# Twelve output-projection steps by block sums in place of ten, and a step's three weight sums in two vector operations

## The chip, the cores and the metric

The kernel runs on one NeuronCore of a Trainium2 chip. Its engines work side by side, each through its own queue in order: TensorE (PE: products; PEld in the profile is its loading of the stationary operand), VectorE (DVE), ScalarE (ACT), GpSimd (POOL) and SyncE (SP), which here only issues transfers. The metric is the device time of one execution in microseconds; runs of one kernel are given with their median.

## The reference

One layer over 256 tokens of width 2048: a normed gated linear attention with its output projection, then a squared-ReLU MLP with 8192 hidden units, then a final norm. Cut to what matters:

```python
h = h + gla(rmsnorm(h)) @ w_out                 # w_out: 2048 x 2048
a = relu(rmsnorm(h) @ w_up)                      # w_up: 2048 x 8192
h = h + (a * a) @ w_down                         # w_down: 8192 x 2048
return rmsnorm(h)
```

All is float32. The kernel splits each weight and each activation into a high part and a low part and forms high x high, low x high and high x low, so that one product of the reference is three products on TensorE.

## The kernel before, in words

The input projections come first (some 288 us), then the output projection (288 to 376 us), then the MLP (376 us to the end).

**The output projection.** `out_group(g, ...)` computes 512 of the 2048 output columns; there are four groups. A group walks over the 2048 input rows in eight steps of 256 rows, in the order `ORDER = (3, 0, 2, 1, 4, 7, 5, 6)`; I call a step by its number kp. A step's weights are a tile `raw` of 128 x 1024: four blocks of 256 columns (row half 0: blocks 0 and 1; row half 1: blocks 2 and 3). A step is done in one of two ways.

- A plain step: one load of 512 KB, one cast to the high part (`copy_hi`, ACT, line 118), one low part (DVE, line 131), then 24 products of 128 x 256 (8 pairs of a stationary and a moving block, three products each).
- A step by sums, a seven-product scheme for a 2 x 2 block product (Strassen's, in the form with few additions): two loads of 256 KB, and an accumulating transfer from POOL's queue that adds block 1 onto block 0 in the tile; a cast and a low part of blocks 1 to 3 (768 columns) and 9 products from them; then three additions on DVE in the same tile (lines 743 to 745), a second cast in two pieces, a second low part (line 761), and 12 products of the sums. That is 7 pairs, 21 products. The second half is held back in `pending` and runs after the next step's products.

The activations need sums too: `turn_pair` makes eight blocks (four sums, four originals; `form_sums`) for the row pairs in `FORMED = (0, 1, 7)`. `summed(g)` says which steps of a group go by sums: 0 and 1 in the first and the last group, 0, 1 and 7 in the two between, ten in all. At the last such step the banks of the sums are copied to `comb` (ACT, lines 767 and 768), combined by four DVE additions (769 to 772), and after the last step two DVE additions (775) write `h`.

**Set in the order of the work.** Each group also turns the last group's `h` by PE transposes at its step 1, copies `h` into the banks of the next group at step 3 (`begin_out`), and squares the last group's `h` at step 4 (`ssq_h`). The high and low parts live in five slots each, taken in turn, so a cast waits until PE has done with the high part five before; `raw` has six buffers. PE's order is fixed by `then_mm`; the order in which ACT and DVE take their work in the output projection is chosen by the compiler's scheduler under a few ordering rules, and each engine then keeps to it. In the MLP `copy_hi` orders ACT's casts too.

**The MLP.** `up` and `down` are generators that alternate: an up step (24 products; low part on DVE at line 165) and a down step, of which 112 of 120 in the interleaved part go by sums in the same way (additions at lines 1088 to 1090, second low part at 1129). The first up steps run alone, right after the output projection. Beside them the last group's `h` is squared (ACT 780), reduced (DVE 803, 804), its root is taken on POOL (356), and DVE writes two diagonals of it, one for each half of the tokens (810, `scale2_diagonals`). PE then makes a row of them (`last_turn`, line 818) and turns the last quarter of `h`. `last_turn` is the ninth entry of `side`, and an up step takes two entries, so PE meets it in the middle of the high products of up step 4.

Of the kernel before, what the change touches and what calls it, by code (L numbers as in the profile page):

```python
# [32 lines left out]
P = 128  # L33
T = 256
# [34 lines left out]
def tile_gla_mlp(ctx, tc, x, xt, cols, w_vg, w_in, w_gate, w_out, w_up, w_down, final_norm, out):  # L69
# [516 lines left out]
                nc.scalar.activation(s, acc[t][c], AF.Silu, scale=r1[:, t : t + 1])  # L586
                nc.vector.tensor_tensor(on[:, t, lo : lo + 512], on[:, t, lo : lo + 512], s, op=ALU.mult)

    S3, S1, S2, S4, A12, A11, A22, A21 = range(8)

    def form_sums(f, sub):
        sub(f[:, S3 : S1 + 1], f[:, A21:].to_broadcast([P, 2, P]), f[:, A11 : A22 + 1])
        sub(f[:, S2], f[:, A11], f[:, S1])
        sub(f[:, S4], f[:, A12], f[:, S2])

    FORMED = (0, 1, 7)
    in_forms = lambda a: a.rearrange("p (f s) -> p f s", f=8)
# [2 lines left out]
    def turn_pair(kp, bank, gain, to):  # L600

        raw_form = raw_forms[kp == 1]
        for i in range(2):
            s = bank[:, i * T : (i + 1) * T].rearrange("p (t s) -> p t s", t=NT)
            nc.scalar.activation(raw_form[:, A12 + 1 - i :: 2], s, AF.Copy, scale=gain(2 * kp + i))
        form_sums(raw_form, lambda o, x, y: nc.vector.tensor_tensor(o, x, y, op=ALU.subtract))
        nc.scalar.copy(to[0], raw_form)
        nc.vector.tensor_tensor(to[1], raw_form, to[0].bitcast(F32), op=ALU.subtract)

# [89 lines left out]
    def out_group(g, order, summed, between):  # L699

        tt = nc.vector.tensor_tensor
        banks = [out_banks[g, t] for t in range(NT)]
        sums_banks = []
        begun = set()
        pending = None
        block = lambda i, n=1: slice(i * T, (i + n) * T)

        def product(bank, o, a, w, n, last=False):
            for x in a[: 2 - n]:
                for d in range(0, w.shape[-1], T):  # L710
                    newest[0] = nc.tensor.matmul(
                        bank[:, o + d : o + d + T], x, w[:, d : d + T],
                        start=bank in sums_banks and bank.name not in begun, stop=last, skip_group_check=True,
                    ).ins
                    begun.add(bank.name)

        def products(these, w, last=False):
            with then_mm():
                for n in range(2):
                    for bank, o, a, c in these:  # L720
                        product(bank, o, a, w[n][:, c], n, last and n == 1)

        for step, kp in enumerate(order):
            by = kp in summed
            raw = raw_tile()[:, : 2 * GT]
            src = w_out[2 * kp * P : 2 * (kp + 1) * P, g * GT : (g + 1) * GT].rearrange("(i p) c -> p i c", p=P)
            if by:
                for i in range(2):
                    last_load[0] = nc.sync.dma_start(out=raw[:, i * GT : (i + 1) * GT], in_=src[:, i])
                nc.gpsimd.dma_start(out=raw[:, :T], in_=src[:, 0, T:], accum_op=ALU.add)  # L730
            else:
                last_load[0] = nc.sync.dma_start(out=raw.rearrange("p (i c) -> p i c", i=2), in_=src)
            w = parts(raw, 2 * GT, slots(), [(T * by, 2 * GT)])
            if by:
                if not sums_banks:
                    sums_banks.extend(psum_bank(i) for i in out_ids[4:])
                f = forms_o(kp)
                at = lambda k, f=f: [a[:, k] for a in f]
                p16, p57 = sums_banks
                products([(p16, 0, at(A11), block(1)), (banks[0], T, at(A12), block(3)), (banks[0], 0, at(S4), block(2))], w)  # L740
                u = raw.rearrange("p (f s) -> p f s", f=4)
                with tc.issue_after(last_lo[0].ins):
                    tt(u[:, 2], u[:, 0], u[:, 2], op=ALU.add)
                    tt(u[:, 1], u[:, 2], u[:, 1], op=ALU.subtract)
                    last = tt(u[:, 3], u[:, 2], u[:, 3], op=ALU.add)
            else:
                for t, i in ((0, 0), (0, 1), (1, 0), (1, 1)):
                    products([(banks[t], 0, row_o(2 * kp + i, t), block(2 * i, 2))], w, step == len(order) - 1 and i == 1)
            if pending:
                pending()  # L750
                pending = None
            if step in between:
                with tc.issue_after(last_hi[0].ins), tc.issue_after(last_lo[0].ins), then_mm():
                    between[step]()
            if by:
                def pending(u=raw, at=at, final=kp == [k for k in order if k in summed][-1]):
                    to = slots()
                    for c in (0, GT):
                        copy_hi(to[0][:, c : c + GT], u[:, c : c + GT])
                    with tc.issue_after(last_lo[0].ins):  # L760
                        last_lo[0] = tt(to[1][:, :G], u, to[0][:, :G].bitcast(F32), op=ALU.subtract)
                    products([
                        (p57, 0, at(S1), block(0)), (p57, T, at(S3), block(1)),
                        (p16, T, at(S2), block(2)), (banks[1], T, at(A22), block(3)),
                    ], to, final)
                    if final:
                        nc.scalar.copy(comb[:, 1:3], two(p16))
                        nc.scalar.copy(comb[:, 0:4:3], two(p57))
                        tt(comb[:, 2], comb[:, 1], comb[:, 2], op=ALU.subtract)
                        tt(comb[:, 0], comb[:, 0], comb[:, 2], op=ALU.subtract)  # L770
                        tt(comb[:, 4], comb[:, 0], comb[:, 3], op=ALU.add)
                        tt(comb[:, 5], comb[:, 2], comb[:, 3], op=ALU.subtract)
        for t in range(NT):
            o = h[:, t, g * GT : (g + 1) * GT].rearrange("p (f s) -> p f s", f=2)
            tt(o, two(banks[t]), comb[:, 4 * t : 4 * t + 2], op=ALU.add)

    def ssq_h(g):
# [3 lines left out]

    ORDER = (3, 0, 2, 1, 4, 7, 5, 6)
    newest[0] = None
    summed = lambda g: FORMED if 0 < g < GROUPS - 1 else FORMED[:2]
    out_group(0, ORDER, summed(0), {
        1: lambda: (turn(on, turned_o, gain_o, 2), turn(on, turned_o, gain_o, 3, forms_o, spare_out(0))),
        3: lambda: begin_out(1),
    })
    hth, htl = (big.tile([P, KT, T], F32R, tag="A" + i, name="h" + i, bufs=1) for i in "hl")
    turned_h = lambda kt: [a[:, kt, :].rearrange("p (t s) -> p t s", t=NT) for a in (hth, htl)]  # L790
    for g in range(1, GROUPS):
        out_group(g, ORDER, summed(g), {
            1: lambda: turn(h, turned_h, g2, g - 1), 4: lambda: ssq_h(g - 1),
            **({3: lambda: begin_out(g + 1)} if g + 1 < GROUPS else {}),
        })
# [126 lines left out]
    def on_vector(i):  # L922
        newest_form[1] = i.ins
# [30 lines left out]
    def forms(m, kp, s):  # L954
        f = form
        on_act(nc.scalar.activation(
            f[:, A12:].rearrange("p (t i) s -> p i t s", t=2), s.rearrange("p i (t s) -> p i t s", t=2), AF.Square
        ))
        if True in ways_of(m, kp):
            form_sums(f, lambda o, x, y: on_vector(nc.vector.tensor_tensor(o, x, y, op=ALU.subtract)))  # L960

    def form_parts(m, kp, act):
        ways = ways_of(m, kp)
# [55 lines left out]
    def down(passes):  # L1019
# [7 lines left out]
        for n, (m, g) in enumerate(passes):  # L1027
# [12 lines left out]
            for kp in range(KP):  # L1040
# [40 lines left out]
                if by_parts:  # L1081
                    these = (P16, 0, at(A11), block(1)), (B32, T, at(A12), block(3)), (B32, 0, at(S4), block(2))
                    u = raw.rearrange("p (f s) -> p f s", f=4)
                    tt = nc.vector.tensor_tensor


                    with tc.issue_after(last_lo[0].ins):
                        tt(u[:, 2], u[:, 0], u[:, 2], op=ALU.add)  # L1088
                        tt(u[:, 1], u[:, 2], u[:, 1], op=ALU.subtract)  # L1089
                        last_sum[0] = tt(u[:, 3], u[:, 2], u[:, 3], op=ALU.add).ins  # L1090
                else:
                    these = [
                        (k, 0, at(f[i]), block(2 * i, 2))
# [15 lines left out]
                def of_sums(u=raw, products=products, at=at, kp=kp, banks=banks, quick=fresh and quick, g=g, then=ahead_of):  # L1109
# [8 lines left out]
                            banks[P57] = begin(P57, g)  # L1118
                    if then and by_sums(*then, 0):
                        ahead = {k: begin(k, then[1]) for k in (B32, P16)}  # L1120
                    for c in (0, GT):
                        copy_hi(to[0][:, c : c + GT], u[:, c : c + GT])
                    if quick and kp == 0:
                        settle(P57)
                        banks[BX4] = begin(BX4, g)
# [1 line left out]
                        settle(BX4)  # L1127
                    with tc.issue_after(last_lo[0].ins):
                        last_lo[0] = nc.vector.tensor_tensor(to[1][:, :G], u, to[0][:, :G].bitcast(F32), op=ALU.subtract)  # L1129
                    early = (P57, 0, at(S1), block(0)), (P57, T, at(S3), block(1))  # L1130
                    late = (P16, T, at(S2), block(2)), (BX4, T, at(A22), block(3))
                    products(0, early, to)
                    yield
                    products(0, late, to)
# [32 lines left out]
    def combine(g):  # L1167
# [4 lines left out]
        def put(t):  # L1172
            hv = h[:, t, g * GT : (g + 1) * GT].rearrange("p (i s) -> p i s", i=2)
            nc.vector.tensor_tensor(hv, hv, e[:, :2], op=ALU.add)  # L1174

        return [
            tt(2, 1, 2, ALU.subtract), tt(0, 0, 2, ALU.subtract), lambda: put(0),
            tt(1, 2, 3, ALU.subtract), tt(0, 0, 3, ALU.add), lambda: put(1),
        ]

    passes = [(m, g) for m in range(ROUNDS) for g in order_of(m) if m < ROUNDS - 1 or g < 2]
# [130 lines left out]
```

## Time and profile before

| | |
|---|---|
| runs | 1044.98 us median of 3 (1044.53 to 1045.18) |
| the profiled execution | 1045.44 us, of which the span from the first to the last instruction is 1043.7 us |
| mean granted TensorE clock | 0.998 |
| busy: PE, DVE, ACT, POOL | 1035.2, 871.1, 721.7, 117.8 us |
| output projection by sums | 10 steps of 32; accumulating transfers 10 |

A busy time is a share of the span only on average: the stages differ. In a row of the timeline stand the start, the time, the engine, the line, the operation, the tiles (out, then in) and how many instructions are merged; in square brackets the time the engine stood idle before, and what released it. PE and DVE overlap one instruction's end with the next one's start, so distances between starts are shorter than durations.

### The profile page before, as it was taken

What the parts mean: (1) busy time and instruction counts of PE and PEld (TensorE: products, weight loads), DVE (VectorE), ACT (ScalarE), POOL (GpSimd) and SP (SyncE); (2) the same over time, 40 slices, a digit from 0 to 9 for tenths busy, and PEclk for the clock granted to TensorE, in tenths of its full rate; (3) what the DMA queues carried; (4) which work ended last, traced back from release to release, by engine and by line L of the source; (5) the groups of instructions that cost most, each with busy time, mean ns of one, the idle gap of its engine ahead of it and who ended that gap; (6) DMA issues with size and microseconds to landing.
All of it is one profiled execution on the core that took longest, in us unless ns stands there. A gap on an engine that the chain in (4) does not pass through costs nothing. (4 is left out here: it accounts for less than half of the span.)

```text
span 1043.7 us, 23272 instructions
## 1 busy us (share of the span) xinstructions
PE 1035.2 (99%) x9064; PEld 1034.3 (99%) x9064; DVE 871.1 (83%) x1287; ACT 721.7 (69%) x1084; POOL 117.8 (11%) x161
## 2 busy tenths in 40 slices
PE   9999999999999999999999999999999999999997
PEld 9999999999999999999999999999999999999997
DVE  5768644656498866889999999999999999999887
ACT  6785544546477755678678688778778777777785
POOL 0000000010011001111111111111111111111100
PEclk9999999999999999999999999999999999999999
DMA  9957665556666686678887887887888888887782
GB/s 333 334 174 208 197 195 170 152 152 182 175 204 189 209 256 190 179 210 226 228 247 230 236 235 217 239 236 223 246 232 222 249 230 228 231 227 225 233 244 89
DMA packets 118414, 226.53 MB, mean 217 GB/s; under 512 B 10608, under 2 KB 26864, under 8 KB 118176
## 3 DMA queue, kind: packets, MB, share of 16 engines
q1 hardware_dynamic: 100064, 207.39, 63.5%
q0 software_dynamic: 17568, 16.00, 10.3%
q8 instruction: 71, 1.16, 0.4%
q10 hardware_dynamic: 672, 1.66, 0.4%
q14 instruction: 39, 0.32, 0.1%
HBM read 222.91 MB, written 2.10 MB: 216 GB/s over the span
## 5 line engine op out<-in xcount | busy, mean ns | idle before, releaser
L118 ACT CAST hi<-raw 128x512 fp32r<-128x512 f32 (+4 forms) x630 | 499.5, 835 | 263.0 <-DVE raw L1089 73.0
L131 DVE TENSOR_TENSOR lo<-raw,hi 128x768 fp32r<-128x768 f32 (+3 forms) x226 | 238.7, 1061 | 90.9 <-ACT hi L118 88.4
L855 PE MATMUL acc<-hi,act 128*128 128x256 f32 x1696 | 247.9, 276 | 0.0
L855 PE MATMUL up<-hh,hi 128*128 128x256 f32 x1024 | 238.8, 277 | 0.0
L855 PE MATMUL up<-hl,hi 128*128 128x256 f32 x1024 | 238.7, 276 | 0.0
L165 DVE TENSOR_TENSOR lo<-raw,hi 128x1024 fp32r<-128x1024 f32 x160 | 195.0, 1221 | 29.9 <-ACT hi L118 29.5
L855 PEld LDWEIGHTS acc<-hi,act 128*128 128x128 f32 x1696 | 217.7, 188 | 0.0
L855 PEld LDWEIGHTS up<-hl,hi 128*128 128x128 f32 x1024 | 192.3, 188 | 0.0
L855 PEld LDWEIGHTS up<-hh,hi 128*128 128x128 f32 x1024 | 192.3, 188 | 0.0
L1065 POOL DMA_DIRECT2D raw<-in_w_down x112 | 97.1, 867 | 518.6 <-DMA raw<-in_w_down 229.8
L1129 DVE TENSOR_TENSOR lo<-raw,hi 128x1024 fp32r<-128x1024 f32 x112 | 136.7, 1220 | 1.3 <-ACT hi L118 1.0
L855 PE MATMUL up<-hh,lo 128*128 128x256 f32 x1024 | 137.0, 276 | 0.0
L855 PE MATMUL acc<-lo,act 128*128 128x256 f32 x848 | 134.1, 276 | 0.0
L855 PEld LDWEIGHTS up<-hh,lo 128*128 128x128 f32 x1024 | 125.7, 188 | 0.0
L855 PEld LDWEIGHTS acc<-lo,act 128*128 128x128 f32 x848 | 113.5, 188 | 0.0
L176 PE MATMUL acc<-hi,xA 128*128 128x256 f32 (+1 forms) x728 | 105.5, 279 | 0.2
L176 PEld LDWEIGHTS acc<-hi,xA 128*128 128x128 f32 x728 | 93.8, 188 | 0.7 <-ACT hi L118 0.6
L176 PE MATMUL acc<-lo,xA 128*128 128x256 f32 (+1 forms) x364 | 60.9, 278 | 0.1
L176 PEld LDWEIGHTS acc<-lo,xA 128*128 128x128 f32 x364 | 50.3, 188 | 0.3 <-DVE lo L131 0.3
L1088 DVE TENSOR_TENSOR raw<-raw 128x256 f32<-128x256 f32 x112 | 47.5, 424 | 2.9
L1089 DVE TENSOR_TENSOR raw<-raw 128x256 f32<-128x256 f32 x112 | 47.5, 424 | 2.8
L219 PE MATMUL acc<-xA,hi 128*128 128x256 f32 x288 | 49.2, 276 | 0.0
(185 smaller groups left out, 1281.9 us busy)
## 6 DMA issues: line engine op xcount, KB each, us to landing
raw<-in_w_up SPq DMA_DIRECT2D x128, 512.0 KB, 4.6
raw<-in_w_down SPq DMA_DIRECT2D x224, 256.0 KB, 4.4
raw<-in_w_in SPq DMA_DIRECT2D x80, 512.0 KB, 3.7
raw<-in_w_down POOLq DMA_DIRECT2D x112, 128.0 KB, 5.1
raw<-in_w_out SPq DMA_DIRECT2D x22, 512.0 KB, 4.7
raw<-in_w_down SPq DMA_DIRECT2D x16, 512.0 KB, 4.8
raw<-in_w_vg SPq DMA_DIRECT2D x14, 520.0 KB, 8.4
raw<-in_w_out SPq DMA_DIRECT2D x20, 256.0 KB, 3.4
```

What stands on the lines that cost most here:

```text
L118: last_hi[0] = nc.scalar.copy(to, raw)
L131: last_lo[0] = nc.vector.tensor_tensor(lo[:, s], raw[:, s], hi[:, s].bitcast(F32), op=ALU.subtract)
L165: last_lo[0] = nc.vector.tensor_tensor(to[1], dst, to[0].bitcast(F32), op=ALU.subtract)
L176: nc.tensor.matmul(o[:, m], x, w[:, m], start=first and c == 0, stop=last, skip_group_check=True)
L219: nc.tensor.matmul(o, u[:, i, s], m, start=kt == 0 and n == 0 and j % 2 == 0, stop=kt == KT - 1 and n == 2, skip_group_check=True,)
L855: newest[0] = nc.tensor.matmul(o, x, w, start=first, stop=last, skip_group_check=True).ins
L1065: nc.gpsimd.dma_start(out=raw[:, :T], in_=src[:, 0, T:], accum_op=ALU.add)
L1088: tt(u[:, 2], u[:, 0], u[:, 2], op=ALU.add)
L1089: tt(u[:, 1], u[:, 2], u[:, 1], op=ALU.subtract)
L1129: last_lo[0] = nc.vector.tensor_tensor(to[1][:, :G], u, to[0][:, :G].bitcast(F32), op=ALU.subtract)
```

## The change

Three things are changed together.

- `summed` is gone: all four groups take steps 0, 1 and 7 by sums, twelve in place of ten. The activation sums of pair 7 were made before too.
- The scheme is written with other signs. `weight_sums` forms block 2 as block 0 minus block 2 in one DVE operation, and blocks 1 and 3, each minus the new block 2, in one operation over two blocks of 256 with the subtrahend repeated. The activation sums (`form_sums`) and the combinations change signs and places, with as many operations as before.
- The second cast takes blocks 0 and 2 first, then 1 and 3 (before: 0 and 1, then 2 and 3), and the products of blocks 0 and 2 come first. The same stands in the MLP's down steps.

```diff
-    S3, S1, S2, S4, A12, A11, A22, A21 = range(8)
-    def form_sums(f, sub):
-        sub(f[:, S3 : S1 + 1], f[:, A21:].to_broadcast([P, 2, P]), f[:, A11 : A22 + 1])
-        sub(f[:, S2], f[:, A11], f[:, S1])
-        sub(f[:, S4], f[:, A12], f[:, S2])
+    S3, S2, S1, S4, A12, A11, A22, A21 = range(8)
+    def form_sums(f, tt):
+        tt(f[:, S3], f[:, A21], f[:, A11], ALU.subtract)
+        tt(f[:, S2 : S1 + 1], f[:, A22 : A22 + 1].to_broadcast([P, 2, P]), f[:, 0::7], ALU.add)
+        tt(f[:, S4], f[:, A12], f[:, S2], ALU.subtract)
+    def weight_sums(u):
+        nc.vector.tensor_tensor(u[:, 2], u[:, 0], u[:, 2], op=ALU.subtract)
+        return nc.vector.tensor_tensor(u[:, 1::2], u[:, 1::2], u[:, 2:3].to_broadcast([P, 2, T]), op=ALU.subtract)
...
                 with tc.issue_after(last_lo[0].ins):
-                    tt(u[:, 2], u[:, 0], u[:, 2], op=ALU.add)
-                    tt(u[:, 1], u[:, 2], u[:, 1], op=ALU.subtract)
-                    last = tt(u[:, 3], u[:, 2], u[:, 3], op=ALU.add)
+                    weight_sums(u)
...
-                    for c in (0, GT):
-                        copy_hi(to[0][:, c : c + GT], u[:, c : c + GT])
+                    for a in range(2):
+                        copy_hi(*(x.rearrange("p (f s) -> p f s", f=4)[:, a::2] for x in (to[0][:, :G], u)))
...
-                        (p57, 0, at(S1), block(0)), (p57, T, at(S3), block(1)),
-                        (p16, T, at(S2), block(2)), (banks[1], T, at(A22), block(3)),
+                        (p57, 0, at(S1), block(0)), (p16, T, at(S2), block(2)),
+                        (p57, T, at(S3), block(1)), (banks[1], T, at(A22), block(3)),
...
-    summed = lambda g: FORMED if 0 < g < GROUPS - 1 else FORMED[:2]
-    out_group(0, ORDER, summed(0), {
+    out_group(0, ORDER, FORMED, {
...
-        out_group(g, ORDER, summed(g), {
+        out_group(g, ORDER, FORMED, {
...
-                        tt(u[:, 2], u[:, 0], u[:, 2], op=ALU.add)
-                        tt(u[:, 1], u[:, 2], u[:, 1], op=ALU.subtract)
-                        last_sum[0] = tt(u[:, 3], u[:, 2], u[:, 3], op=ALU.add).ins
+                        last_sum[0] = weight_sums(u).ins
...
-                    early = (P57, 0, at(S1), block(0)), (P57, T, at(S3), block(1))
-                    late = (P16, T, at(S2), block(2)), (BX4, T, at(A22), block(3))
+                    early = (P57, 0, at(S1), block(0)), (P16, T, at(S2), block(2))
+                    late = (P57, T, at(S3), block(1)), (BX4, T, at(A22), block(3))
```

More of the change, by code (lines that the diff above doesn't have):

```diff
@@ L605, in turn_pair @@
             nc.scalar.activation(raw_form[:, A12 + 1 - i :: 2], s, AF.Copy, scale=gain(2 * kp + i))
-        form_sums(raw_form, lambda o, x, y: nc.vector.tensor_tensor(o, x, y, op=ALU.subtract))
+        form_sums(raw_form, lambda o, x, y, op: nc.vector.tensor_tensor(o, x, y, op=op))
         nc.scalar.copy(to[0], raw_form)
@@ L768, in pending @@
                         nc.scalar.copy(comb[:, 0:4:3], two(p57))
-                        tt(comb[:, 2], comb[:, 1], comb[:, 2], op=ALU.subtract)
+                        tt(comb[:, 2], comb[:, 1], comb[:, 2], op=ALU.add)
                         tt(comb[:, 0], comb[:, 0], comb[:, 2], op=ALU.subtract)
-                        tt(comb[:, 4], comb[:, 0], comb[:, 3], op=ALU.add)
-                        tt(comb[:, 5], comb[:, 2], comb[:, 3], op=ALU.subtract)
+                        tt(comb[:, 4], comb[:, 0], comb[:, 3], op=ALU.subtract)
+                        tt(comb[:, 5], comb[:, 2], comb[:, 3], op=ALU.add)
         for t in range(NT):
@@ L959, in forms @@
         if True in ways_of(m, kp):
-            form_sums(f, lambda o, x, y: on_vector(nc.vector.tensor_tensor(o, x, y, op=ALU.subtract)))
+            form_sums(f, lambda o, x, y, op: on_vector(nc.vector.tensor_tensor(o, x, y, op=op)))
     def form_parts(m, kp, act):
@@ L1083, in down @@
                     u = raw.rearrange("p (f s) -> p f s", f=4)
-                    tt = nc.vector.tensor_tensor
                     with tc.issue_after(last_lo[0].ins):
-                        tt(u[:, 2], u[:, 0], u[:, 2], op=ALU.add)
-                        tt(u[:, 1], u[:, 2], u[:, 1], op=ALU.subtract)
-                        last_sum[0] = tt(u[:, 3], u[:, 2], u[:, 3], op=ALU.add).ins
+                        last_sum[0] = weight_sums(u).ins
                 else:
@@ L1120, in of_sums @@
                         ahead = {k: begin(k, then[1]) for k in (B32, P16)}
-                    for c in (0, GT):
-                        copy_hi(to[0][:, c : c + GT], u[:, c : c + GT])
+                    for a in range(2):
+                        copy_hi(*(x.rearrange("p (f s) -> p f s", f=4)[:, a::2] for x in (to[0][:, :G], u)))
                     if quick and kp == 0:
@@ L1176, in combine @@
         return [
-            tt(2, 1, 2, ALU.subtract), tt(0, 0, 2, ALU.subtract), lambda: put(0),
-            tt(1, 2, 3, ALU.subtract), tt(0, 0, 3, ALU.add), lambda: put(1),
+            tt(2, 1, 2, ALU.add), tt(0, 0, 2, ALU.subtract), lambda: put(0),
+            tt(1, 2, 3, ALU.add), tt(0, 0, 3, ALU.subtract), lambda: put(1),
         ]
```

## The prediction

> **What bounds the kernel now.** I read the page's busy times, then the waits of PE's weight loads, then busy times by window.
>
> ```profile
> PE 1035.2 (99%) x9064; PEld 1034.3 (99%) x9064; DVE 871.1 (83%) x1287; ACT 721.7 (69%) x1084; POOL 117.8 (11%) x161
> ```
>
> ```profile
> PEld aux L252 <- DVE ones L249: 1.1, 1, 1.1
> PEld acc L176 <- ACT hi L118: 0.6, 2, 0.3
> PEld acc L176 <- DVE lo L131: 0.3, 1, 0.3
> ```
>
> ```profile
> 300.00:360.00 60.00, 60.00 (x530) 60.00 (x530) 53.51 (x81) 40.50 (x67) 6.14 (x7) 1.00 0.74 213
> 500.00:600.00 100.00, 100.00 (x885) 100.00 (x884) 96.44 (x148) 74.86 (x113) 17.32 (x20) 1.00 0.83 234
> ```
>
> PE is the bound. All its waits for another engine add up to 2.0 us, all of them on lines of the input projections; in the output projection (first window) and in the MLP (second) it has no gap at all, at clock 1.00. So every product taken out is worth its whole time, and every new PE wait is paid whole. DVE is next: 96.44 of 100 us in the MLP. A window's columns after its length are PE, PEld, DVE, ACT, POOL.
>
> **The change part by part. Two more steps by sums.** Step 7 of the first and of the last group now takes 9 + 12 products in place of 24, so six products go. Group 3's products before:
>
> ```profile
> 363.22 0.84 PE L711 MATMUL acc<-hi,of 128*128 128x256 f32 x6
> 363.90 0.50 PE L711 MATMUL acc<-lo,of 128*128 128x256 f32 x3
> 364.24 0.39 PE L711 MATMUL acc<-hi,oth 128*128 128x256 f32 x2
> ...
> 371.04 0.39 PE L711 MATMUL acc<-hi,oth 128*128 128x256 f32 x2
> ...
> 373.76 0.39 PE L711 MATMUL acc<-hi,oth 128*128 128x256 f32 x2
> ...
> 376.48 0.28 PE L855 MATMUL up<-hh,hi 128*128 128x256 f32 x1
> ```
>
> A plain step lasts 373.76 − 371.04 = 2.72 us for 24 products, 0.1133 each; nine take 364.24 − 363.22 = 1.02, the same distance. Six products are 0.68 us: the gain. The Trainium skill, "TensorE: Matmul & The Clock Gate", section "Back-to-back issue gap", gives N/2.4 + 2.5 ns for a lone product and calls it no measure for a stream with weight loads; at N = 256 it would be 109.2 ns, the gain 0.655 and the time 0.025 us higher. The trace's 113.3 ns decides.
>
> **Their loads.** One load of 512 KB becomes two of 256 KB and an accumulating one.
>
> ```profile
> raw<-in_w_out SPq DMA_DIRECT2D x22, 512.0 KB, 4.7
> raw<-in_w_out SPq DMA_DIRECT2D x20, 256.0 KB, 3.4
> raw<-in_w_out POOLq DMA_DIRECT2D x10, 128.0 KB, 4.5
> ```
>
> 4.7 us becomes 3.4 + 4.5 for the sums, which are wanted only after the next step's 24 products. The tile comes free some 5 us later than a plain one (after the second low part), and whatever SP queues for it moves back: in group 0 a load of group 1, wanted about 8 us after it would land, in group 3 that of up step 4, which PE wants 10.9 us into the MLP and which would land at 0.5. Cost nothing; cover 8 and 10 us.
>
> **The weight sums in two operations.**
>
> ```profile
> 282.05 0.42 DVE L743 TENSOR_TENSOR raw<-raw 128x256 f32<-128x256 f32 x1
> 282.51 0.42 DVE L744 TENSOR_TENSOR raw<-raw 128x256 f32<-128x256 f32 x1
> 282.85 0.42 DVE L745 TENSOR_TENSOR raw<-raw 128x256 f32<-128x256 f32 x1
> ...
> 287.99 2.49 DVE L587 TENSOR_TENSOR on<-on,some 128x512 f32<-128x512 f32 x4
> 335.07 0.69 DVE L775 TENSOR_TENSOR h<-acc,some 128x512 f32<-128x512 f32 x1
> ```
>
> Before: 0.46 to the dependent second, 0.34 to the third, 0.42 for it: 1.22 us. After: 0.46 and one of 512 elements, 0.69, or 0.60 where another follows ((2.49 − 0.69) / 3). A step saves some 0.08 us, 112 + 10 steps about 9 us of DVE. None of that is on the path: PE never waits for it. Its price if the new form runs otherwise is the third rival's.
>
> **The cast of blocks 0 and 2 first** costs as much as that of 0 and 1. It could help only where PE waits for a half cast, and there is no such wait. But it is built in another order: in the output projection the scheduler now takes blocks 0 and 2 of step 7's sums, then one to three casts of later steps, then blocks 1 and 3. What PE waits for is the last piece and the low part behind it. I followed each group from E, the end of step 7's first nine products. Closest is group 2, where DVE's low parts of later steps come ahead of the combinations and of the `h` that PE turns in group 3:
>
> ```profile
> 308.35 1.14 ACT L118 CAST hi<-raw 128x512 fp32r<-128x512 f32 x2 [1.71 <-PE acc L711]
> ...
> 334.21 0.95 DVE L131 TENSOR_TENSOR lo<-raw,hi 128x768 fp32r<-128x768 f32 x1
> ...
> 380.16 1.22 DVE L165 TENSOR_TENSOR lo<-raw,hi 128x1024 fp32r<-128x1024 f32 x1
> 381.29 0.28 DVE L810 TENSOR_SCALAR work<-ident,r 128x128 f32<-128x128 f32 x1
> ...
> 336.50 1.04 PE L616 MATMUL aux<-ident,h 128*128 128x128 f32 x8
> ```
>
> The last cast piece ends at E + 1.22; four low parts of 1024 (what follows one starts 1.13 to 1.14 behind it: 380.16, 381.29) and one of 768 (0.86 to 0.88), four combinations and one sum at 0.34, a two-block sum at 0.60 and the two `h` additions (0.60, 0.69) end at E + 10.29. PE comes to the turn after 2.72 + 1.36 + 2.72 + 2.72 + 1.02 = E + 10.54. Spare 0.25 us, where before it was 336.50 − (335.07 + 0.69) = 0.74. Group 3's low part of step 6 has 0.70 to spare, that of step 7's sums 0.94, groups 0 and 1 over 1.1. So nothing is lost, but the cover is thin: second rival.
>
> **The entrance to the MLP.** Here the built order changes most. Before, DVE's two diagonals (line 810) came around one low part; now the combinations and `h` additions of group 3 are spread between the low parts of up steps, and so reduce, scale and the diagonals stand behind the low part of up step 7 (counted from 0), and the second diagonal behind that of step 8 as well. PE wants both in the middle of up step 4, ahead of the row product.
>
> ```profile
> 378.91 0.16 DVE L803 TENSOR_REDUCE ms<-hs 128x2 f32<-128x8 f32 x1 [0.15 <-ACT sq L780]
> 379.11 0.17 DVE L804 TENSOR_SCALAR ms<-ms 128x2 f32<-128x2 f32 x1
> 379.96 0.29 DVE L810 TENSOR_SCALAR work<-ident,r 128x128 f32<-128x128 f32 x1 [0.68 <-POOL r L356]
> ...
> 385.01 1.22 DVE L165 TENSOR_TENSOR lo<-raw,hi 128x1024 fp32r<-128x1024 f32 x1 [1.49 <-ACT hi L118]
> 387.73 1.23 DVE L165 TENSOR_TENSOR lo<-raw,hi 128x1024 fp32r<-128x1024 f32 x1 [1.50 <-ACT hi L118]
> ```
>
> ```profile
> 381.21 1.05 ACT L118 CAST hi<-raw 128x1024 fp32r<-128x1024 f32 x1 [1.39 <-PE up L855]
> 383.93 1.05 ACT L118 CAST hi<-raw 128x1024 fp32r<-128x1024 f32 x1 [1.67 <-PE up L855]
> 386.65 1.05 ACT L118 CAST hi<-raw 128x1024 fp32r<-128x1024 f32 x1 [1.67 <-PE up L855]
> ```
>
> ```profile
> 388.26 0.60 PE L818 MATMUL row<-work,ones 128*128 128x128 f32 x4
> ```
>
> Call U the start of the first up step (376.48 before). Those casts, of up steps 6, 7 and 8, start at U + 4.73, 7.45 and 10.17; each waits for a high part's slot that PE frees at the end of the high products of up steps 1, 2 and 3. Because the releaser is PE, the times stand to U as before. So in the changed kernel the low part of step 7 lasts from U + 8.53 to 9.75, reduce and scale end near 10.1, the root takes POOL to 10.7 as before (0.68 us after the scale), the first diagonal is written, and the low part of step 8 runs U + 11.25 to 12.48 because its cast ends at 11.22. The second diagonal starts 1.13 behind that low part's start (as from 380.16 to 381.29) and ends at U + 12.67; with some 0.07 to reach PE, 12.74. PE reaches the row product at 388.26 − 376.48 = U + 11.78 and its second half, two of four products later, at 12.0. PE then stands 0.74 us: no slack behind it, so it is paid whole. The turn, row copy and high parts behind it move with PE.
>
> **The sum.** The profiled execution, 1045.44, − 0.68 + 0.74 = 1045.50. It lay 0.46 above the median of the runs, so against 1044.98: 1045.04, rounded 1045.05. PE would then be 0.34 early from group 0 on, 0.68 early at the MLP's start, and 0.06 late after up step 4.
>
> **The rivals.** A comparison of this kernel can tell about 0.2% (2.1 us) from no change; that is my bound.
>
> First, *the row product isn't late*: the diagonals come in time because a low part of DVE runs earlier than I built it, and the bare saving is left: 1044.98 − 0.68 = 1044.30. For it: the wait hangs on one cast (386.65) being tied to a slot. Against: that row names PE as releaser and nothing in the change frees the slot sooner.
>
> Second, *the split cast starves PE in the output projection* (the other side). If the chain behind E is x later than I have it, group 2's turn loses x − 0.25 and group 3's step 6 and sums x − 0.70 and x − 0.94, groups 0 and 1 from 1.1 on. At x = 1.3, about one low part or one cast more in the way, 1.05 + 0.60 + 0.36 and more is 2.0 us, and it counts as slower; from 1045.5 to 1047.8. For it: a chain of eleven operations on DVE with 0.25 us to spare. Against: every one of them is costed from a row.
>
> Third, *the two-block operation runs slowly* because its repeated operand and its skipped blocks are read less well.
>
> ```profile
> L1088 DVE TENSOR_TENSOR raw<-raw 128x256 f32<-128x256 f32 x112 | 47.5, 424 | 2.9
> L960 DVE TENSOR_TENSOR work<-work 128x256 f32<-128x256 f32 x30 | 12.6, 421 | 0.1
> ```
>
> ```profile
> 700.12 0.62 PE L855 MATMUL acc<-hi,act 128*128 128x256 f32 x4
> ...
> 705.22 0.62 PE L855 MATMUL acc<-hi,act 128*128 128x256 f32 x4
> ```
>
> An up and a down step take 5.10 us, so 100 us hold 19.6, and DVE's idle 3.56 us (500 to 600) is 0.18 a step; with 0.08 saved, the operation may take 0.60 + 0.26 = 0.86 us before DVE becomes the bound. At half speed, 1.20, each of 112 steps loses 0.34: 38 us, about 1083. Against it: line 960 already has a repeated operand of two blocks and takes 421 ns, as the plain 424. The Trainium skill, "VectorE: DVE Perf Modes", section "Mode 1× (REGULAR) — the baseline", says that fp32 runs one element a cycle whatever the stride; the two rows agree.
>
> **How the numbers follow.** The forecast, 0.68: it rests on an order that is fixed and on a cast tied to PE. The bare saving 0.15. The starved output projection 0.11, about half of it beyond 0.2%. The slow operation 0.03. Left over 0.03: slower by something unseen 0.01, faster by over 0.2% 0.02, for which there is no mechanism as PE has nothing else to give. So faster 0.02; same 0.68 + 0.15 + 0.05 = 0.88; slower 0.06 + 0.03 + 0.01 = 0.10. The range takes the forecast and the bare saving with the spread of the runs below it (1044.30 − 0.4) and the starved case to x = about 1: 1043.9 to 1046.2.
>
> **What would show it.** PE has 9058 products; step 7 in groups 0 and 3 has 9 + 12. The waits list a new one, PE's row or its weight load on DVE's `work`, of 0.6 to 0.8 us, about 12 us into the MLP; none there speaks for the first rival. Any wait of PE in the output projection (on `hi`, `lo` or `h`) is the second rival. DVE's two-block sums take 687 ns, and its busy time falls by about 9 us; over 0.86 us it is the third. A span that falls or rises by over 2 us makes me wrong.

## The result

| | runs | median | lowest to highest |
|---|---|---|---|
| before | 5 | 1044.98 us | 1044.53 to 1045.65 |
| changed | 5 | 1048.95 us | 1048.64 to 1049.55 |

The changed kernel is slower by 3.97 us: 1.0038 times the time before, 95% interval 1.0024 to 1.0053. The forecast was 1045.05, the range 1043.9 to 1046.2; it was wrong.

### The profile page after: what moved, and what is told of

Same layout as the page of the kernel before. It is cut to its first block, busy times and chain, and to the rows that moved or that the text cites. A ratio compares the mean times of both kernels' runs of the same rounds, so it can differ in the third digit from the quotient of the medians.

```text
span 1047.2 us, 23156 instructions
## 1 busy us (share of the span) xinstructions
PE 1036.4 (99%) x9058; PEld 1034.6 (99%) x9058; DVE 864.0 (83%) x1171; ACT 735.8 (70%) x1088; POOL 119.5 (11%) x163
## 4 chain that ended last, share of the span: by engine, by line
PE 97%; ACT 1%; issue 1%; DMA 1%; DVE 0%; SPq 0%; POOLq 0%; POOL 0%; DVEq 0%; ACTq 0%
PE up L856 33%; PE acc L856 28%; PE acc L176 18%; PE acc L715 8%; PE acc L219 6%; PE aux L219 2%; PE aux L176 1%; PE aux L620 1%; PE aux L521 1%; DMA raw<-in_w_vg 1%; ACT hi L118 0%; DVE lo L763 0%; ACT sqf L1196 0%; SPq L168 0%; DVE lo L165 0%
## 5 line engine op out<-in xcount | busy, mean ns | idle before, releaser
L118 ACT CAST hi<-raw 128x512 fp32r<-128x512 f32 (+4 forms) x634 | 510.1, 834 | 231.7 <-PE acc L176 64.1
L598 DVE TENSOR_TENSOR raw<-raw 128x512 f32<-128x512 f32 x124 | 85.5, 690 | 3.1
L597 DVE TENSOR_TENSOR raw<-raw 128x256 f32<-128x256 f32 x124 | 52.4, 423 | 2.8
```

Source lines behind the costliest of these rows:

```text
L118: last_hi[0] = nc.scalar.copy(to, raw)
L597: nc.vector.tensor_tensor(u[:, 2], u[:, 0], u[:, 2], op=ALU.subtract)
L598: return nc.vector.tensor_tensor(u[:, 1::2], u[:, 1::2], u[:, 2:3].to_broadcast([P, 2, T]), op=ALU.subtract)
```

## The profile after

The page's busy times of the changed kernel:

```profile
PE 1036.4 (99%) x9058; PEld 1034.6 (99%) x9058; DVE 864.0 (83%) x1171; ACT 735.8 (70%) x1088; POOL 119.5 (11%) x163
```

PE has six products fewer, as the change says, and is yet busy 1.2 us longer. The waits of PE's weight loads (who waited for whom: us in total, times, longest):

```profile
PEld acc L715 <- DVE lo L763: 1.3, 2, 0.7
PEld aux L252 <- DVE ones L249: 1.1, 1, 1.1
PEld acc L715 <- ACT hi L118: 1.0, 1, 1.0
PEld acc L176 <- ACT hi L118: 0.8, 2, 0.6
PEld row L819 <- DVE work L811: 0.7, 1, 0.7
```

Line 715 is the output projection's product, line 763 the low part of a step's sums, lines 819 and 811 the row product and the diagonals. Before, none of these three groups was there. On PE's timeline they are four places:

```profile
350.38 0.28 PE L715 MATMUL acc<-hi,otl 128*128 128x256 f32 x1
351.06 0.74 PE L715 MATMUL acc<-lo,oth 128*128 128x256 f32 x4 [0.41 <-DVE lo L763]
...
372.87 0.28 PE L715 MATMUL acc<-hi,otl 128*128 128x256 f32 x1
373.99 0.38 PE L715 MATMUL acc<-hi,oth 128*128 128x256 f32 x1 [0.85 <-ACT hi L118]
...
375.25 0.74 PE L715 MATMUL acc<-lo,oth 128*128 128x256 f32 x4 [0.52 <-DVE lo L763]
...
391.10 0.38 PE L819 MATMUL row<-work,ones 128*128 128x128 f32 x2
391.97 0.49 PE L819 MATMUL row<-work,ones 128*128 128x128 f32 x2 [0.49 <-DVE work L811]
392.30 0.93 PE L620 MATMUL aux<-ident,h 128*128 128x128 f32 x7
```

The sums of step 7 in group 2 (351), the same in group 3 twice (374 and 375), and the row product (392). The starts of the same work in both timelines tell how much each stretch lost:

| PE starts | before | changed | difference | lost or won since the line above |
|---|---|---|---|---|
| first step by sums, group 0 | 290.87 | 290.43 | −0.44 | |
| first step by sums, group 1 | 313.78 | 313.00 | −0.78 | −0.34: three products of group 0 |
| sums of step 1, group 2 | 345.26 | 344.48 | −0.78 | 0 |
| first step by sums, group 3 | 357.16 | 357.49 | +0.33 | +1.11 |
| sums of step 1, group 3 | 366.96 | 367.43 | +0.47 | +0.14 |
| first up step | 376.48 | 378.85 | +2.37 | +1.90: 2.24 lost, 0.34 won |
| row product | 388.26 | 391.10 | +2.84 | +0.47 |
| last turn | 388.71 | 392.30 | +3.59 | +0.75 |
| last steps (line 176) | 1014.59 | 1018.18 | +3.59 | 0 |

From the first line on, the loss is 4.03 us, which agrees with the medians' 3.97 (the 0.44 ahead of it lies in the input projections, which the change doesn't touch; it is about the 0.46 us by which the profiled execution of the kernel before lies above its median). It is −0.68 + 1.25 (group 2 and what follows) + 2.24 (group 3) + 0.47 + 0.75. The MLP behind the turn costs the same in both kernels.

**Where the waits come from.** ScalarE and VectorE around the first wait, group 2 of the changed kernel:

```profile
341.69 0.61 ACT L118 CAST hi<-raw 128x512 fp32r<-128x512 f32 x1
...
345.98 0.62 ACT L118 CAST hi<-raw 128x512 fp32r<-128x512 f32 x1 [2.30 <-PE acc L715]
...
349.13 0.61 ACT L118 CAST hi<-raw 128x512 fp32r<-128x512 f32 x1
```

```profile
342.33 1.23 DVE L763 TENSOR_TENSOR lo<-raw,hi 128x1024 fp32r<-128x1024 f32 x1 [1.54 <-ACT hi L118]
343.48 2.09 DVE L131 TENSOR_TENSOR lo<-raw,hi 128x768 fp32r<-128x768 f32 x2
345.48 0.42 DVE L597 TENSOR_TENSOR raw<-raw 128x256 f32<-128x256 f32 x1
345.93 0.69 DVE L598 TENSOR_TENSOR raw<-raw 128x512 f32<-128x512 f32 x1
349.78 1.23 DVE L763 TENSOR_TENSOR lo<-raw,hi 128x1024 fp32r<-128x1024 f32 x1 [3.15 <-PE acc L715]
```

The cast at 341.69 is the second piece (blocks 1 and 3) of step **1**'s sums. Its first piece ran at 339.48, and the casts of step 7 and of step 5 stand between them on ScalarE. VectorE stands idle 1.54 us for it, then makes its low part (342.33), then two low parts that stand behind it, and only then, at 345.48, the sums of step **7**. Their first piece is cast at 345.98, three casts of later steps follow, and the second piece comes at 349.13. The last low part runs to 351.01, and PE takes it at 351.06. So a late piece delays the next step's sums and then its own successor's piece: the lag is handed on from step to step.

Two of these rows name PE as the releaser, where I read VectorE's sum and ScalarE's piece. The cast at 345.98 starts 0.08 us after the sum of block 2 ends (345.48 + 0.42), and the low part at 349.78 starts 0.04 us after the second piece ends (349.13 + 0.61). Further down, in the run with the changed work in the program's order, PE's products stand at the same times to within 0.05 us, and yet the same cast starts at 342.12, again 0.08 us after the sum of block 2, and the same low part at 344.47, again 0.04 us after the second piece, there with the cast named as the releaser. So the sum and the piece fix these two starts, not a product of PE.

In the kernel before both pieces of step 7 in group 2 run together, and earlier:

```profile
344.41 1.14 ACT L118 CAST hi<-raw 128x512 fp32r<-128x512 f32 x2 [1.95 <-issue]
```

In group 3 of the changed kernel the lag is larger. The second piece of step 7 starts at 373.33; PE stops after four products of the sums, goes on at 373.99, released by the cast itself, and stops again for the low part.

```profile
373.33 0.61 ACT L118 CAST hi<-raw 128x512 fp32r<-128x512 f32 x1
```

## The experiments

Three theories. **A**: the queue order is the cause, namely the second piece standing behind later casts. **B**: twelve steps are more work than ScalarE and VectorE can do in time. **C**: the two-operation sums or the new cast order starve PE whatever the number of steps.

### Ten steps again

```diff
-    out_group(0, ORDER, FORMED, {
+    out_group(0, ORDER, summed(0), {
...
-        out_group(g, ORDER, FORMED, {
+        out_group(g, ORDER, summed(g), {
```

> The changed kernel with ten steps by sums again; the two-operation sums and the cast of blocks 0 and 2 first are kept. Theory A (the second cast piece, queued on ScalarE behind casts of later steps, holds up the low part, the next sums and then PE): in the built order of this kernel the two pieces stand together in every group, so PE does not wait in the output projection; 1045.0 +- 0.4, like before. Theory B (twelve steps are simply more work than ScalarE and VectorE can do in time): also 1045.0. Theory C (the two-operation sums or the new cast order starve PE by themselves): waits in groups 1 and 2, 1046 to 1048.

1045.44 us (ratio to before 1.0004, 0.9995 to 1.0013): no difference that can be told. PE has no wait in the output projection. C falls: the same sums and casts do no harm with ten steps. The page's busy times of the kernel with ten steps:

```profile
PE 1034.6 (99%) x9064; PEld 1034.1 (99%) x9064; DVE 862.2 (83%) x1165; ACT 734.1 (70%) x1084; POOL 117.8 (11%) x161
```

Its group of the two-block sums (busy us, mean ns of one, idle before):

```profile
L598 DVE TENSOR_TENSOR raw<-raw 128x512 f32<-128x512 f32 x122 | 84.2, 690 | 3.2
```

871.1 has become 862.2, 8.9 us less, and the two-block operation takes 690 ns: off the path and worth nothing there.

### Twelve steps alone

```diff
-    summed = lambda g: FORMED if 0 < g < GROUPS - 1 else FORMED[:2]
+    summed = lambda g: FORMED
```

> The kernel before with twelve steps by sums and nothing else. Theory A: here too the built order puts the second cast piece of step 7 of groups 2 and 3 two or three casts behind the first, so PE waits in both groups and at the row product: 1048 to 1050. Theory B: the same, 1048 to 1050, or more since three sums cost more than two operations. Theory C: no waits, 1044.3.

1057.28 us (1.0116, 1.0102 to 1.0130): slower by 12.3 us, far beyond the 1048 to 1050 that A gave (B had left room for more). The same kind of waits, longer ones:

```profile
PEld acc L711 <- ACT hi L118: 4.3, 3, 2.0
PEld acc L711 <- DVE lo L761: 3.6, 5, 0.7
...
PEld row L818 <- DVE work L810: 0.7, 1, 0.7
PEld aux L616 <- DVE h L775: 0.4, 2, 0.2
```

9.0 us of waits. The rest is in part TensorE's clock. In windows of 1 us (columns after the length: PE, PEld, DVE, ACT, POOL busy, then the clock and the DMA):

```profile
379.00:380.00 1.00, 0.18 (x2) 0.00 (x0) 0.00 (x0) 1.00 (x2) 0.00 (x0) 1.00 0.43 166
380.00:381.00 1.00, 0.07 (x1) 0.07 (x1) 0.09 (x1) 1.00 (x3) 0.00 (x0) 1.00 0.02 6
381.00:382.00 1.00, 0.68 (x4) 0.47 (x4) 1.00 (x1) 0.83 (x1) 0.00 (x0) 1.00 0.00 0
382.00:383.00 1.00, 0.81 (x4) 0.81 (x5) 1.00 (x2) 0.78 (x1) 0.00 (x0) 0.66 0.00 0
383.00:384.00 1.00, 1.00 (x7) 1.00 (x7) 1.00 (x2) 1.00 (x3) 0.00 (x0) 0.50 0.81 141
384.00:385.00 1.00, 1.00 (x6) 1.00 (x6) 1.00 (x2) 0.24 (x1) 0.00 (x0) 0.50 0.89 332
385.00:386.00 1.00, 1.00 (x8) 1.00 (x7) 1.00 (x2) 0.00 (x0) 0.00 (x0) 0.63 1.03 387
```

After 2.3 us of idle time in four, the granted clock is halved for some 3.4 us, which costs about 1.7 us by my estimate from these rows. The Trainium skill, "TensorE: Matmul & The Clock Gate", section "HAM oscillation — how this bites in real kernels", gives idle gaps over about 3.4 us as what brings the half clock. Here no single gap reached that (the longest wait is 2.0 us), and the clock fell. So the rule as a limit for one gap doesn't cover this row.

A and B both expected waits here; what this run adds is that at twelve steps the old sums and casts, in the order that the scheduler gives them, are 8.3 us slower than the new ones in theirs.

### Twelve steps with the old pieces

```diff
-                    for a in range(2):
-                        copy_hi(*(x.rearrange("p (f s) -> p f s", f=4)[:, a::2] for x in (to[0][:, :G], u)))
+                    for c in (0, GT):
+                        copy_hi(to[0][:, c : c + GT], u[:, c : c + GT])
...
-                        (p57, 0, at(S1), block(0)), (p16, T, at(S2), block(2)),
-                        (p57, T, at(S3), block(1)), (banks[1], T, at(A22), block(3)),
+                        (p57, 0, at(S1), block(0)), (p57, T, at(S3), block(1)),
+                        (p16, T, at(S2), block(2)), (banks[1], T, at(A22), block(3)),
```

> The changed kernel, twelve steps and two-operation sums, with the second cast in the output projection taken as blocks 0, 1 and then 2, 3 and the products in that order, as before; the MLP as changed. Both pieces then wait for the same operation and stand together in the built order; the diagonals stand one low part earlier. Theory A: no waits of PE in the output projection and none at the row product; 1044.3 +- 0.4. Theory B: PE waits as in the changed kernel, 1047.5 to 1049. Theory C: in between, if the cast order is the cause, 1044.3, if the two-operation sums are, 1047 and above.

1044.31 us (0.9993, 0.9985 to 1.0002), 4.64 us less than the changed kernel, and what A gave. All waits of PE's weight loads in it:

```profile
PEld aux L252 <- DVE ones L249: 1.1, 1, 1.1
PEld acc L176 <- ACT hi L118: 0.5, 2, 0.3
```

None is left in the output projection or at the row product. ScalarE and VectorE in the same place, group 2:

```profile
338.88 1.14 ACT L118 CAST hi<-raw 128x512 fp32r<-128x512 f32 x2 [0.17 <-DVE raw L598]
...
344.72 2.10 ACT L118 CAST hi<-raw 128x512 fp32r<-128x512 f32 x3 [1.78 <-PE acc L715]
```

```profile
340.06 1.23 DVE L763 TENSOR_TENSOR lo<-raw,hi 128x1024 fp32r<-128x1024 f32 x1 [0.47 <-ACT hi L118]
...
343.50 0.42 DVE L597 TENSOR_TENSOR raw<-raw 128x256 f32<-128x256 f32 x1
```

Both pieces of step 1 run together at 338.88, its low part at 340.06 instead of 342.33, and the sums of step 7 at 343.50 instead of 345.48. B falls: the twelve steps' work fits.

### The changed work in the program's order

```diff
     newest[0] = None
+    ordered[0] = True
```

> The changed kernel with ScalarE's casts of the output projection kept in the order in which the program lists them, which is done in the MLP in any case; work and operands are the same as in the changed kernel. The second piece then follows the first. Theory A: 1044.3 +- 0.5, no wait of PE in groups 2 and 3. Theory B: 1047.5 to 1049, the waits stay, since no work is taken out. Theory C: 1047 and above.

1044.49 us (0.9995, 0.9986 to 1.0004), no wait in the output projection. Same operations, operands and pieces as in the changed kernel; only the order of ScalarE's casts differs (and VectorE's behind them). This is the cleanest test of A: 4.46 us are order alone.

### The second cast in one piece

```diff
-                    for a in range(2):
-                        copy_hi(*(x.rearrange("p (f s) -> p f s", f=4)[:, a::2] for x in (to[0][:, :G], u)))
+                    copy_hi(to[0][:, :G], u)
```

> The changed kernel with the second cast of the output projection taken whole, in one operation of 1024 columns. Theory A: no piece can be left behind, so PE has no wait in groups 2 and 3; the diagonals stand as in the kernel with the old cast; 1044.3 +- 0.4. Theory B (the work of twelve steps is too much): 1047.5 to 1049. If the first products of the sums need the early start that the split gives, a wait on the whole cast at each sums step of some tenths of a us, 1045 to 1048.

1044.17 us (0.9993, 0.9984 to 1.0002). The split isn't needed in the output projection at all; PE doesn't miss the early start.

### Order kept in the last group only

```diff
     for g in range(1, GROUPS):
+        ordered[0] = g == GROUPS - 1
```

> The changed kernel with ScalarE's casts kept in the program's order in the last group alone. In the built order the second piece of step 7 is then late in groups 0, 1 and 2 only, and the diagonals stand one low part earlier. Theory A: the waits of group 3 (2.24 us), the slow products after them (0.47) and the row wait (0.75) go, that of group 2 (1.25) stays: 1048.95 - 3.46 = 1045.5. Theory B: group 3 still waits, 1047 to 1049.

1045.46 us (1.0004, 0.9995 to 1.0012), against 1045.5 expected. The 3.46 us of group 3 and of the entrance to the MLP go, and group 2's 1.25 stay: the terms of the table add up.

### Twelve steps, old sums, program's order

```diff
-    summed = lambda g: FORMED if 0 < g < GROUPS - 1 else FORMED[:2]
+    summed = lambda g: FORMED
+    ordered[0] = True
```

> The kernel before with twelve steps and ScalarE's casts of the output projection in the program's order; sums in three operations and the cast as before. Theory A: what made twelve steps slow (1057.3) is the late second piece alone, 1044.3 +- 0.5. Theory B (twelve steps need the two-operation sums): PE still waits, 1046 to 1055.

1044.25 us (0.9993, 0.9985 to 1.0002). One line of order takes 13 us from the kernel of the twelve steps alone. The old sums in three operations do as well as the new ones.

### The last turn later

```diff
-    side.extend([nothing] * 3 + [scale2, nothing, scale2_diagonals] + [nothing] * 2 + [last_turn])
+    side.extend([nothing] * 3 + [scale2, nothing, scale2_diagonals] + [nothing] * 4 + [last_turn])
```

> The changed kernel with the last turn two entries later in the list that the up steps work off, so PE meets the row product one up step (2.72 us) later; nothing else. Theory A (the row wait is a loss of its own, beside those of the output projection): the wait at the row product goes, the other waits stay; 1048.95 - 0.75 = 1048.2. Rival (the row wait only passes on what was late before it): 1048.9. If the slower distance of products after a wait (0.1178 us in place of 0.1133) ends with the turn, it lasts one up step longer and costs 0.1 us of the gain.

The wait at the row product is gone, the others stand as before. But the seven executions fall in two groups, four from 1048.14 to 1048.70 and three from 1056.53 to 1057.49. The lower ones are near the 1048.2 expected, though the gain there, about 0.4 us, is less than 0.75; the upper ones were expected by nobody. The profile is of one of these, and it has no new wait in it. PE is busy without a gap and does fewer products (three stretches of 20 us of this kernel, columns as above):

```profile
400.00:420.00 20.00, 20.00 (x172) 20.00 (x171) 13.64 (x18) 10.60 (x13) 2.62 (x3) 1.00 0.72 198
...
600.00:620.00 20.00, 20.00 (x172) 20.00 (x171) 18.96 (x26) 15.04 (x22) 3.45 (x4) 1.00 0.83 231
640.00:660.00 20.00, 20.00 (x179) 20.00 (x179) 18.79 (x24) 16.98 (x26) 2.59 (x3) 1.00 0.79 226
```

172 products in 20 us, 0.117 to 0.118 us each, up to about 625 us; then 179; the kernel before has 178 or 179 in these stretches. Some 240 us with 7 of 179 products lost is 9 us. The granted clock reads 1.00 in both.

### One wait of known length

To see what a wait costs by itself, I took the kernel of the old pieces, which has none, and let PE come to the row product too early.

```diff
-    side.extend([nothing] * 3 + [scale2, nothing, scale2_diagonals] + [nothing] * 2 + [last_turn])
+    side.extend([nothing] * 3 + [scale2, nothing, scale2_diagonals] + [last_turn])
```

> The kernel of e3 (no waits) with the last turn two entries earlier in the list of the up steps, so PE meets the row product one up step sooner, at U + 9.06, its second half at 9.28, while the second diagonal ends at U + 10.19 as in e3. One wait of about 1.0 us and no other. If a wait costs its length: 1044.3 + 1.0 = 1045.3. If PE's products run at the slower distance (0.1178 us for 0.1133, 0.1 us more for each up step) for a while after any wait: 0.3 us more if it lasts 8 us as in group 2 of the changed kernel, up to 9 us more if it lasts 240 us as in the profiled execution of e5.

1045.48 us (1.0005, 0.9996 to 1.0014), 1.17 more than without the wait.

```diff
-    side.extend([nothing] * 3 + [scale2, nothing, scale2_diagonals] + [nothing] * 2 + [last_turn])
+    side.extend([nothing] + [scale2, nothing, scale2_diagonals] + [last_turn])
```

> As e9, with the norm's sums two entries and the last turn four entries earlier: PE meets the row product at U + 6.34, and the diagonals end near U + 8.5. One wait of about 2.0 us. If a wait costs its length: 1044.3 + 2.0 = 1046.3. With a slower distance after it: 0.3 to 9 us more; if the slow stretch grows with the wait, more than behind the wait of e9.

1048.15 us (1.0028, 1.0018 to 1.0039; 1046.70 to 1048.68), 3.84 more than without. The one row of each that tells the wait:

```profile
385.60 0.49 PE L819 MATMUL row<-work,ones 128*128 128x128 f32 x2 [0.80 <-DVE work L811]
```

```profile
383.94 0.92 PE L819 MATMUL row<-work,ones 128*128 128x128 f32 x4 [1.97 <-DVE work L811]
```

From the first up step to the turn the shorter wait cost 1.06 us and the longer 2.43 by the starts in the two timelines; in the profiled executions 0.48 and 0.22 more were lost behind the turn, where products stood 0.118 us apart up to about 402 and 393 us. So in the profiled executions a wait cost more than its length: about 1.5 us for the shorter one, which the list of waits gives as 1.0, and 2.65 for the longer one of 2.0.

The 3.84 us of the longer wait's median hold something else besides. Three of its seven executions have a mean granted clock of 0.998 (1046.70 to 1047.48 us), the other four one of 0.996 or 0.997 (1048.15 to 1048.68 us). A stretch of 3.4 us at half clock, as in the kernel of the twelve steps alone, would lower the mean by 0.0016 and cost 1.7 us, which is about what sets the four apart. The profiled execution is one of the three, at a clock of 1.00 around the wait, and no trace of the four was kept; so that the clock fell in them is likely and not shown. That the slow stretch grows with the wait isn't shown either: it ended sooner behind the longer one.

## Why the prediction was wrong, point by point

- **PE is the bound, every new wait is paid whole.** Right, and by more than whole.
- **Six products are 0.68 us.** Right. Where nothing waits, the twelve steps bring −0.65, −0.47, −0.82 and −0.74 us against the runs of before beside them (old pieces, program's order, one cast, twelve ordered). None of the four can be told from no change by its interval alone; the table of starts shows the 0.34 us of group 0 directly.
- **Loads hidden.** Right: none of PE's waits comes from one.
- **Two operations for three save about 9 us of VectorE, off the path.** Right: 8.9 with ten steps, 690 ns for the new form, no gain in time. The third rival (a slow form) fell.
- **The cast order.** This step failed. It read: "The last cast piece ends at E + 1.22". E, the end of step 7's nine direct products in group 2, is 346.86 in the changed kernel; the piece starts at 349.13 and ends near 349.7, E + 2.9, about 1.65 us later. In group 3, where E is 369.81, the piece ends near 373.94, E + 4.1, some 2.9 us later. I saw that the second piece of step 7 was queued behind later casts, but followed each group "from E, the end of step 7's first nine products". Three casts stand between the pieces in group 2, and they run back to back from 346.50, with the second and the third not yet begun at E. E + 1.22 has no room for them; it needs a first piece that comes well ahead of E, as in the kernel before, where E is 347.64 in group 2 and the pieces run from 344.41 to 345.55. In the changed kernel the first piece starts at 345.98, 0.9 us ahead of E. Step 1's second piece was queued behind later casts too, and through VectorE's order it moved the sums of step 7, the very start of the chain. So the second rival is what happened, with x about 1.65 in group 2 and 2.9 in group 3, beyond the 1.3 that I had priced. It also bit in another place than I had ranked first: at the last products of the sums themselves, whose spare I had put at 0.94 in group 3 (2.9 less 0.94 is 2.0 of the 2.24 us lost there), and not at the turn. There `h` came late too, at 358.76 or E + 11.9 in place of E + 10.29, but PE had by then lost 1.15 us itself, came to the turn at 358.55 (E + 11.69, not 10.54), and no wait of the turn is listed. (By its list the chain to the turn has thirteen operations, not eleven; its sum holds.)
- **The row product: 0.74 us.** Right in place and size: 0.75 from the starts (391.10 to 392.30, less the 0.45 that the four products took before). Both sides came some 0.4 us later after the first up step than I had them, PE at U + 12.25 and the second diagonal's end at U + 13.07, because the products ran slower; the cast being tied to PE kept the difference. With the diagonals one low part earlier, as with the old pieces, it doesn't occur; the first rival was wrong for this order.
- **The sum.** 1045.05 lacked 1.25 + 2.24 + 0.47 us. Of the 4.71 us lost in all, PE's weight loads waited 3.0 (1.3 + 1.0 + 0.7); the other 1.7 are products further apart after the waits, for which the prediction had no term: some 0.8 at the distance of 0.118 us, most of the rest in single distances of 0.2 us and more within about a microsecond of the three waits of the output projection.
- **The chance.** 0.11 for the starved output projection was too low for a chain that I had costed from one point in its middle.

Why the compiler's scheduler puts the pieces apart when group 0 also has three steps by sums, and together when both pieces hang on the same operation, isn't shown; that the order it chose is the loss is.

## What to carry to other kernels

An operation split in two pieces has two places in a queue, and the second may end up behind work that is wanted later; check in the built order what stands between them, and tie them together if nothing needs the first one early. Follow such a chain from where its first link became ready, back over the step before it, and not from a fixed point in the bound engine's schedule. And when the bound engine has no gap at all, count more for a new gap than its length.

## What the runs showed of the hardware

After a wait of PE its products stand further apart for a while, 0.1178 us in place of 0.1133, at a granted clock of 1.00. In the changed kernel it lasts from the wait of group 3 to the row product, 376 to 391 us; the start distance of two up steps' low products is 2.83 us, where 24 products took 2.72 before:

```profile
383.56 1.10 PE L856 MATMUL up<-hh,lo 128*128 128x256 f32 x8
386.39 1.10 PE L856 MATMUL up<-hh,lo 128*128 128x256 f32 x8
```

It lasted about 7 us after the wait in group 2 (351 to the turn at 358.5), 7 after the single wait of 2 us, some 15 after that of 1 us, and about 240 in one execution of the kernel with the later turn.

A wait is not the only thing that goes with it. In the kernel before the eleven products behind a turn of `h` stand 0.12 us apart (from 389.70 on, where nothing waited), and from about 24 to 63 us, in the input projections, the products stand 0.118 apart: in the row below, 169 in 20 us with PE busy throughout at clock 1.00. The other kernels show the same in both places.

```profile
30.00:50.00 20.00, 20.00 (x169) 20.00 (x168) 13.80 (x19) 14.33 (x19) 1.07 (x2) 1.00 0.90 317
```

DMA and VectorE are no clear mark of it: the stretch at 400 us of the kernel with the later turn has less of both than that at 640, which runs at the usual distance. What starts and ends it stays open. That the clock was halved with no single wait above 2.0 us is told with the twelve steps alone.
